# One fused transformer block pair: the expert stage gathers and adds only the slots in use, and adds whole 4 KB rows

## The chip, the cores and the metric

The kernel runs as one program on one core of a Trainium2 chip. The metric is the device time of one execution in microseconds (us). The engines named below are TensorE (PE in the rows, its weight loads PEld), VectorE (DVE), ScalarE (ACT), GpSimd (POOL) and SyncE (SP), and the core's 16 DMA engines, which every queue shares: q1 is the queue on which SP issues the weight loads, q0 the one on which GpSimd issues its indirect transfers.

## The reference, cut to what matters

A first block (a mixer of dilated attention and gated linear attention, then a mixture of experts) is followed by a second block (pooling and an RWKV recurrence). The change touches the mixture of experts alone:

```
T = 512 tokens, D = 1024, 32 experts, top 4 of each token
logits = xt @ router_w + router_b
top_v, top_i = top_k(logits, 4);  gates = softmax(top_v)
for each expert e, over the tokens that chose it:
    gu  = x[tokens] @ w_gate_up[e] + b_gate_up[e]          # 1024 x 2048
    act = min(gu[::2], 7) * sigmoid(1.702 * ..) * (clip(gu[1::2], -7, 7) + 1)
    out = act @ w_down[e] + b_down[e]                       # 1024 x 1024
    y[tokens] += gate * out
```

All is float32. An expert has 8 MB of gate-and-up weights and 4 MB of down weights, so 32 experts are 384 loads of 1 MB. On the reference's inputs the experts get 200, 146, 133, 125, 109, 86, 82, 82, 78, 76, 72, 65, 58, 57, 55, 54, 51, 48, 48, 48, 44, 42, 41, 40, 38, 37, 32, 26, 25, 16 and 13 tokens, and expert 31, which the kernel always takes first, 21.

## The kernel before, in words

The first part (to about 350 us) computes the mixer, its output projection and the router. Expert 31 is started before the routing is known (`FIXED`, three groups of 32 slots, computed by `counted` and `routing`); the other experts are sorted by their token counts, and rank r gets a fixed number of slots, `CAPS[r]`. `groups` cuts these into groups of m = 64 or m = 32 slots: 50 groups, 35 of 64 and 15 of 32, 2720 slots in all. A loop behind the planned part (`rest`) would compute tokens for which `CAPS` was too small.

A group passes these steps. `tokens` builds on VectorE a 0/1 matrix P (slot against token), TensorE multiplies it with a table to get for each slot the token's row and gate, VectorE turns them into an index tile `ix`, and GpSimd issues an indirect DMA (L1073) that gathers m rows of 4 KB of the normed activations into `xg`, which holds two groups, at partitions 0 and 64. Column 0 of `ix` is the row to gather, column 1 the row to add to; an empty slot points to one of 64 padding rows. `xT` transposes `xg` on TensorE (L1096) and ScalarE copies it out (L1098). `products` (L1120, L1123) multiplies by 1024 of the 2048 gate-and-up columns; the group has m stationary columns, and the 128/m column tiles of TensorE work on 128/m shares of the weight columns side by side, so the result lies as 128 partitions x 512 (m = 64) or 128 x 256 (m = 32). `gating` forms the activation, `actT` transposes it, `down` (L1166, L1172) does the last product in the same layout, ScalarE evicts it with the gate as scale into `o` (L1174), and GpSimd issues an indirect DMA that adds it into the accumulator in HBM (L1177): 128 descriptors, of 2 KB for m = 64, of 1 KB for m = 32.

TensorE's order is written by hand: `SEQ` lists 96 phases, (rank, phase) with phase 0 and 1 for the two halves of gate-and-up and 2 for down, interleaved over ranks. The weights of a phase are four loads of 1 MB on SP (L1037), in the same order, into a ring of 16 tiles; a load is issued only when the load four before it has landed (`FLIGHT`) and when its tile is free. `prep` runs `tokens` ahead of a rank's first phase by 40 units of a cost table, 8 for a group of 64 and 5 for one of 32. The other engines are ordered by a scheduler. The adds form a chain: each waits until the one before has landed. After the last add the accumulator is read back (L1455, `ym<-accd`) and the second block runs.

Of the kernel before, what the change touches and what calls it, by code (L numbers as in the profile page):

```python
# [10 lines left out]
F32 = mybir.dt.float32  # L11
# [4 lines left out]
AF = mybir.ActivationFunctionType  # L16
OP = mybir.AluOpType
# [64 lines left out]
def pre(tc, A, g):  # L82
# [294 lines left out]
    t4 = lambda name: prB.tile([128, 1024], F32, name=name, tag="t4", bufs=2)  # L377
    G = K()

    def gates():  # L380
# [46 lines left out]
    def dense():  # L427
# [39 lines left out]

        G.gates = 0

# [124 lines left out]
    prt_.__exit__(None, None, None)  # L594


CAPS = [96] + [224, 160, 160, 128, 128, 128] + [96] * 6 + [64] * 16 + [32] * 3
FIXED = 31
SEQ = [divmod(i, 3) for i in (
# [4 lines left out]
assert len(CAPS) == 32 and sorted(SEQ) == [(r, p) for r in range(32) for p in range(3)]  # L604


def groups(cap, first=False):
    if first:
        return [(s, 32) for s in range(0, cap, 32)]
    out, s = [], 0  # L610
    while s < cap:
        m = 64 if cap - s >= 64 else 32
        out.append((s, m))
        s += m
    return out

# [4 lines left out]
def route_consts():  # L621
# [395 lines left out]
class Moe:  # L1017
    def __init__(self, tc, A, g, work, ps, wtile):
        self.tc, self.A, self.g, self.w, self.ps, self.wtile = tc, A, g, work, ps, wtile
        self.nc = tc.nc  # L1020
        self.lead = 40
        self.ngu = 0
        self.half = 0
        self.loads, self.flow = [], True


# [20 lines left out]
        return [x for j in range(4) for x in self.load1(e, ph, j)]  # L1047


    def tokens(self, pos, aux, s0, m, gates=True):  # L1050
        nc, g, w, ps, c2 = self.nc, self.g, self.w, self.ps, self.g.c2
        dup = 128 // m
        T = pos.shape[1]
        P = w.tile([128, T, dup, m], BF, name="P", tag="P")
        nc.vector.tensor_tensor(P, c2("iota1")[:, None, None, s0:s0 + m].to_broadcast([128, T, dup, m]),
                                pos[:, :, :, None].to_broadcast([128, T, dup, m]), op=OP.is_equal)
        inf = ps.tile([128, 6], F32, name="inf", tag="tr", bufs=2)
        n = 6 if gates else 3
        for t in range(T):
            nc.tensor.matmul(inf[:, 0:n], P[:, t].rearrange("p d m -> p (d m)"), aux[:, t, 0:n], start=(t == 0), stop=(t == T - 1))  # L1060
        f = w.tile([128, 2], F32, name="inff", tag="inff", bufs=4)
        ix = w.tile([128, 2], I32, name="ix", tag="ix", bufs=14)

        nc.vector.tensor_reduce(out=f[:, 0:1], in_=inf[:, 0:2], axis=AX.X, op=OP.add)  # L1064
        nc.vector.tensor_copy(ix[:, 0:1], f[:, 0:1])  # L1065
        nc.vector.scalar_tensor_tensor(f[:, 1:2], inf[:, 2:3], c2(f"npad{m}"), c2(f"pad{m}"), op0=OP.mult, op1=OP.add)

        h = self.half
        if h == 0:
            self.xg = w.tile([128, 1024], F32, name="xg", tag="xg", bufs=3)  # L1070
        xg = self.xg[h:h + m]
        self.half = 64 - h
        nc.gpsimd.indirect_dma_start(out=xg, out_offset=None, in_=g.h2d[0:64 + 128 * T], in_offset=bass.IndirectOffsetOnAxis(ap=ix[0:m, 0:1], axis=0))  # L1073
        nc.vector.tensor_add(f[:, 0:1], f[:, 0:1], f[:, 1:2])
        nc.vector.scalar_tensor_tensor(ix[:, 1:2], f[:, 0:1], float(dup), c2(f"dg{m}"), op0=OP.mult, op1=OP.add)
        G = dict(m=m, xg=xg, h=h, ix=ix, P=P)
        if gates:
            self.gates(G, None, inf)
        return G
# [10 lines left out]

    def xT(self, G):
        nc, g, w, ps = self.nc, self.g, self.w, self.ps
        m, h = G['m'], G['h']
        pt = ps.tile([128, 8, m], F32, name="ptx", tag="tr", bufs=2)
        for k in range(8):
            nc.tensor.transpose(pt[:, k, :], G['xg'][:, k * 128:(k + 1) * 128], g.ident[h:h + m, h:h + m])  # L1096
        xT = w.tile([128, 8, m], F32, name="xT", tag="xT", bufs=7)
        nc.scalar.copy(xT, pt)  # L1098
        G['xT'] = xT

    def products(self, G, W, hf, sel):
        nc, g, ps = self.nc, self.g, self.ps
        m = G['m']
        cg = 128 // m
        n = 1024 // cg
        self.ngu += 1
        p = G['p', hf] = ps.tile([128, 512], F32, name="pgu", tag="mm" if self.ngu % 4 else "po", bufs=3 if self.ngu % 4 else 1)

        def part(w, c):

            if m == 64:
                return w[:, c * n:(c + 1) * n]
            return w.rearrange("p (a i k two) -> p a k i two", a=2, k=2, two=2)[:, c // 2, c % 2]

        def to(c):
            o = p[c * m:(c + 1) * m, :n]
            return o if m == 64 else o.rearrange("p (i two) -> p i two", two=2)

        for c in range(cg):
            nc.tensor.matmul(to(c), sel.to_broadcast([96, m]), part(g.bp[:, hf * 1024:(hf + 1) * 1024], c), start=True, stop=False)  # L1120
        for k in range(8):
            for c in range(cg):
                nc.tensor.matmul(to(c), G['xT'][:, k, :], part(W[k], c), start=False, stop=(k == 7))  # L1123
            yield

    def gating(self, G, hf):
# [32 lines left out]
    def down(self, G, W, sel, hold=False):  # L1159
        nc, g, w, ps = self.nc, self.g, self.w, self.ps  # L1160
        m = G['m']
        dg = 128 // m
        n = 1024 // dg
        p = ps.tile([128, 512], F32, name="pdn", tag="s", bufs=2)
        for c in range(dg):
            nc.tensor.matmul(p[c * m:(c + 1) * m, :n], sel.to_broadcast([96, m]), g.bp[:, 2048 + c * n:2048 + (c + 1) * n], start=True, stop=False)  # L1166
        for k in range(8):
            hf, q = k // 4, k % 4
            aT = G['aT', hf]
            lhs = aT[:, q % 2, (q // 2) * 64:(q // 2) * 64 + 64] if m == 64 else aT[:, 0, q * 32:(q + 1) * 32]  # L1170
            for c in range(dg):
                nc.tensor.matmul(p[c * m:(c + 1) * m, :n], lhs, W[k][:, c * n:(c + 1) * n], start=False, stop=(k == 7))  # L1172
        o = w.tile([128, 512], F32, name="o", tag="o", bufs=2)
        nc.scalar.activation(o[:, :n], p[:, :n], AF.Copy, scale=G['gate'][:, 0:1])  # L1174

        def add():
            return nc.gpsimd.indirect_dma_start(out=g.acc.rearrange("r (d n) -> (r d) n", n=n),  # L1177
                                                out_offset=bass.IndirectOffsetOnAxis(ap=G['ix'][:, 1:2], axis=0),
                                                in_=o[:, :n], in_offset=None, compute_op=OP.add)
        if hold:  # L1180
            self.held = add
        else:
            self.added = add()

    def run(self, moves):
        g, nc, ps = self.g, self.nc, self.ps
# [7 lines left out]

        T, W = {0: g.ahead}, {(0, 0): g.first[0], (0, 1): g.first[1], (0, 2): g.first[2]}

        cost = [sum((8 if m == 64 else 5) for _, m in groups(CAPS[r], r == 0)) for r, _ in SEQ]
        when = np.concatenate([[0], np.cumsum(cost)])
        first = {r: i for i, (r, ph) in enumerate(SEQ) if ph == 0}

        def prep(i):
            for x in sorted(first, key=first.get):
                if x not in T and when[first[x]] - when[i] <= self.lead:
                    T[x] = [self.tokens(g.ppr[:, :, x:x + 1], g.aux[:, :, x, :], s0, m) for s0, m in groups(CAPS[x])]

        def transposes(j):
            if j < len(SEQ) and SEQ[j][1] == 0:
# [1147 lines left out]
```

## Time and profile before

| | |
|---|---|
| median of 3 runs | 1835.36 us (1834.03 to 1836.15) |
| profiled execution, its own time | 1837.41 us |
| its span, first to last instruction | 1835.6 us |
| granted TensorE clock, mean | 0.952 |
| PE, DVE, ACT, POOL busy | 91%, 35%, 23%, 14% |
| HBM read, written | 494.05 MB, 26.36 MB |

The span has three parts. To about 400 us the mixer and the routing run; from 400 to 1440 us the experts; after that the second block. The profile gives for any stretch the busy time of each engine, the share of the 16 DMA engines and what they moved, the packets of each queue, and who waited for whom. A packet of a queue is what one DMA engine moves at a time; the share of a queue is the sum of its packets' times over the time of 16 engines.

### The profile page before, as it was taken

Reading aid. Unit: us, or ns where it says so; the run is one execution under the profiler, and the core shown is the slowest. Engines: PE = TensorE matmul, PEld = TensorE weight load, DVE = VectorE, ACT = ScalarE, POOL = GpSimd, SP = SyncE. Lnnn points to the kernel's source line nnn. Section 1 sums busy time; section 2 is a strip of 40 time slices with the busy share of each in tenths; the row PEclk is TensorE's granted clock in tenths of the full one; section 3 lists DMA queues with packets and bytes.
Section 4 is the critical chain, followed back from the end, with each engine's and each line's share of the span. In section 5 each row is a group of like instructions: output and inputs, shape, how many; then the busy total and the mean of one; then the engine's idle time right before and its main releaser. Section 6 shows DMA issues by size and latency. Waiting matters only on the chain. (4 is left out here: it accounts for less than half of the span.)

```text
span 1835.6 us, 28333 instructions
## 1 busy us (share of the span) xinstructions
PE 1669.5 (91%) x11329; PEld 892.5 (49%) x11329; DVE 648.7 (35%) x1639; ACT 420.4 (23%) x866; POOL 261.2 (14%) x189
## 2 busy tenths in 40 slices
PE   6889898989999999899998999999997489969988
PEld 4666576744333333233333333334332267757766
DVE  4636746642212111121211211212111367954353
ACT  4445554311111010011111011101011254322231
POOL 1734621011111001100110101020110100000000
PEclk9989889999999999999999999999999689979989
DMA  9654326799999999999999999999999934320151
GB/s 330 183 162 140 117 104 228 263 323 394 392 391 392 389 392 389 381 389 395 383 387 391 346 414 393 393 376 388 391 369 392 328 101 107 111 70 7 47 165 71
DMA packets 183961, 522.28 MB, mean 285 GB/s; under 512 B 28730, under 2 KB 71636, under 8 KB 167316
## 3 DMA queue, kind: packets, MB, share of 16 engines
q1 hardware_dynamic: 162562, 491.31, 71.0%
q0 software_dynamic: 10720, 22.29, 5.6%
q10 hardware_dynamic: 10546, 6.85, 1.3%
q8 instruction: 90, 1.47, 0.3%
q14 instruction: 43, 0.35, 0.1%
HBM read 494.05 MB, written 26.36 MB: 284 GB/s over the span
## 5 line engine op out<-in xcount | busy, mean ns | idle before, releaser
L1123 PE MATMUL pgu<-wra,xT 128*64 128x512 f32 (+1 forms) x1784 | 295.7, 522 | 11.1 <-DMA wra<-in_w_gate_up_dram 9.4
L1123 PE MATMUL pgu<-wrb,xT 128*32 128x256 f32 (+1 forms) x1936 | 281.9, 499 | 10.4 <-DMA wrb<-in_w_gate_up_dram 9.1
L1134 DVE TENSOR_SCALAR gm<-pgu 128x256 f32<-128x256 f32 (+1 forms) x100 | 38.4, 384 | 672.7 <-PE pgu L1123 672.7
L1123 PEld LDWEIGHTS pgu<-wra,xT 128*64 128x64 f32 (+1 forms) x1784 | 99.2, 127 | 172.6 <-issue 136.4
L1123 PEld LDWEIGHTS pgu<-wrb,xT 128*32 128x32 f32 (+1 forms) x1936 | 98.8, 125 | 162.5 <-issue 120.3
L1172 PE MATMUL pdn<-wra,aT 128*64 128x512 f32 (+1 forms) x1144 | 164.2, 488 | 1.6 <-DMA wra<-in_w_down_dram 1.5
L1177 POOL DMA_INDIRECT accd<-o,ix x50 | 78.7, 1574 | 606.9 <-ACT aT L1156 410.0
L1135 ACT ACTIVATE sg<-gm 128x256 f32<-128x256 f32 (+1 forms) x100 | 38.7, 387 | 357.3 <-DVE gm L1134 353.5
L1172 PE MATMUL pdn<-wrb,aT 128*64 128x512 f32 (+1 forms) x688 | 108.8, 505 | 6.8 <-DMA wrb<-in_w_down_dram 6.7
L1073 POOL DMA_INDIRECT xg<-h2d,ix x50 | 48.5, 970 | 406.7 <-DVE ix L1065 115.4
L1172 PEld LDWEIGHTS pdn<-wra,aT 128*64 128x64 f32 (+1 forms) x1144 | 58.3, 123 | 89.7 <-issue 71.8
L1174 ACT ACTIVATE o<-pdn,gate 128x512 f32<-128x512 f32 (+1 forms) x50 | 31.2, 624 | 276.4 <-PE pdn L1172 247.9
L1156 ACT COPY aT<-pta 128x256 f32<-128x256 f32 (+1 forms) x100 | 31.2, 341 | 268.0 <-PE pta L1154 267.5
L1507 PE MATMUL pf<-hh,wfh 128*128 128x512 f32 (+1 forms) x208 | 86.7, 417 | 0.5 <-ACT hh L1494 0.5
L1508 PE MATMUL pf<-hh,wfl 128*128 128x512 f32 (+1 forms) x208 | 83.0, 399 | 2.2 <-DVE wfl L1351 2.2
L1509 PE MATMUL pf<-hl,wfh 128*128 128x512 f32 (+1 forms) x208 | 82.6, 397 | 0.5 <-DVE hl L1495 0.5
L1123 PE MATMUL pgu<-wrx,xT 128*64 128x512 f32 (+1 forms) x440 | 69.3, 505 | 3.7 <-ACT xT L1098 2.1
L1064 DVE TENSOR_REDUCE inff<-inf 128x1 f32<-128x2 f32 x50 | 7.6, 152 | 174.4 <-PE inf L1060 167.8
L1172 PEld LDWEIGHTS pdn<-wrb,aT 128*64 128x64 f32 (+1 forms) x688 | 35.9, 126 | 68.2 <-issue 51.3
L1154 PEld LDWEIGHTS pta<-ct,act 128*128 128x128 f32 x170 | 24.2, 196 | 56.1 <-issue 52.6
L1507 PEld LDWEIGHTS pf<-hh,wfh 128*128 128x128 f32 x208 | 40.8, 196 | 12.1 <-issue 2.0
L1508 PEld LDWEIGHTS pf<-hh,wfl 128*128 128x128 f32 x208 | 40.8, 196 | 11.5 <-DVE wfl L1351 2.5
(514 smaller groups left out, 2531.5 us busy)
## 6 DMA issues: line engine op xcount, KB each, us to landing
wra<-in_w_gate_up_dram SPq DMA_DIRECT2D x125, 1024.0 KB
wrb<-in_w_gate_up_dram SPq DMA_DIRECT2D x104, 1024.0 KB
wra<-in_w_down_dram SPq DMA_DIRECT2D x63, 1024.0 KB
wrb<-in_w_down_dram SPq DMA_DIRECT2D x48, 1024.0 KB
wrx<-in_w_gate_up_dram SPq DMA_DIRECT2D x27, 1024.0 KB
wst<-in_w_in_dram SPq DMA_DIRECT2D x49, 512.0 KB
wrx<-in_w_down_dram SPq DMA_DIRECT2D x17, 1024.0 KB
wmb<-in_w_mod_dram SPq DMA_DIRECT2D x32, 512.0 KB
```

The costliest lines, as they stand in the source:

```text
L1073: nc.gpsimd.indirect_dma_start(out=xg, out_offset=None, in_=g.h2d[0:64 + 128 * T], in_offset=bass.IndirectOffsetOnAxis(ap=ix[0:m, 0:1], ax ...
L1123: nc.tensor.matmul(to(c), G['xT'][:, k, :], part(W[k], c), start=False, stop=(k == 7))
L1134: nc.vector.tensor_scalar(gm[:, :h], pv[:, :, 0], 7.0, None, op0=OP.min)
L1135: nc.scalar.activation(sg[:, :h], gm[:, :h], AF.Sigmoid, scale=1.702)
L1154: nc.tensor.transpose(pt[:, f, :], G['act', hf][:, f:128 * fh:fh], g.ident)
L1156: nc.scalar.copy(aT[:, 0:fh], pt[:, 0:fh])
L1172: nc.tensor.matmul(p[c * m:(c + 1) * m, :n], lhs, W[k][:, c * n:(c + 1) * n], start=False, stop=(k == 7))
L1174: nc.scalar.activation(o[:, :n], p[:, :n], AF.Copy, scale=G['gate'][:, 0:1])
L1177: return nc.gpsimd.indirect_dma_start(out=g.acc.rearrange("r (d n) -> (r d) n", n=n), out_offset=bass.IndirectOffsetOnAxis(ap=G['ix'][:, 1 ...
L1507: nc.tensor.matmul(p[:, a], hi[:, k, :], hh[:, k, a], start=(k == 0), stop=False)
L1508: nc.tensor.matmul(p[:, a], lo[:, k, :], hh[:, k, a], start=False, stop=False)
L1509: nc.tensor.matmul(p[:, a], hi[:, k, :], hl[:, k, a], start=False, stop=(k == 7))
```

## The change

`CAPS` gets a finer table, in multiples of 8; `groups` yields (start, m, used). The 50 groups stay 50, but now 32 of m = 64 and 18 of m = 32: the second group of rank 6 and the groups of ranks 27 and 28 go from 64 to 32. The slots in use are 2224: by group size 64 (19 groups), 56 (3), 48 (7), 40 (3), 32 (6), 24 (4), 16 (4) and 8 (4). Only the used slots are gathered, transposed and multiplied by gate-and-up; the unused part of P is set to zero. The column tiles keep their size and place. The down product is unchanged, but ScalarE evicts it in 128/m pieces that put the shares of a row side by side, so that a slot's result is one row of 1024 in one partition; `o` becomes one tile with two halves, partitions 0 to 63 and 64 to 127, used in turn. The add carries one descriptor of 4 KB for each used slot.

```diff
-CAPS = [96] + [224, 160, 160, 128, 128, 128] + [96] * 6 + [64] * 16 + [32] * 3
+CAPS = ([96] + [200, 152, 136, 128, 112, 88, 88, 88, 80, 80, 72, 72] + [64] * 2 + [56] * 3 + [48] * 6 + [40] * 3 + [32] * 3 + [16] * 2)
...
-        m = 64 if cap - s >= 64 else 32
-        out.append((s, m))
+        m = 64 if cap - s > 32 else 32
+        out.append((s, m, min(m, cap - s)))
...
-        nc.vector.tensor_tensor(P, c2("iota1")[:, None, None, s0:s0 + m].to_broadcast([128, T, dup, m]),
-                                pos[:, :, :, None].to_broadcast([128, T, dup, m]), op=OP.is_equal)
+        nc.vector.tensor_tensor(P[:, :, :, 0:used], c2("iota1")[:, None, None, s0:s0 + used].to_broadcast([128, T, dup, used]),
+                                pos[:, :, :, None].to_broadcast([128, T, dup, used]), op=OP.is_equal)
+        if used < m:
+            nc.vector.memset(P[:, :, :, used:m], 0.0)
...
-        xg = self.xg[h:h + m]
+        xg = self.xg[h:h + used]
         self.half = 64 - h
-        nc.gpsimd.indirect_dma_start(out=xg, out_offset=None, in_=g.h2d[0:64 + 128 * T], in_offset=bass.IndirectOffsetOnAxis(ap=ix[0:m, 0:1], axis=0))
-        nc.vector.tensor_add(f[:, 0:1], f[:, 0:1], f[:, 1:2])
-        nc.vector.scalar_tensor_tensor(ix[:, 1:2], f[:, 0:1], float(dup), c2(f"dg{m}"), op0=OP.mult, op1=OP.add)
+        nc.gpsimd.indirect_dma_start(out=xg, out_offset=None, in_=g.h2d[0:64 + 128 * T], in_offset=bass.IndirectOffsetOnAxis(ap=ix[0:used, 0:1], axis=0))
+        nc.vector.tensor_add(ix[:, 1:2], f[:, 0:1], f[:, 1:2])
...
-                nc.tensor.matmul(to(c), G['xT'][:, k, :], part(W[k], c), start=False, stop=(k == 7))
+                nc.tensor.matmul(to(c, used), G['xT'][:, k, :], part(W[k], c), start=False, stop=(k == 7))
...
-        o = w.tile([128, 512], F32, name="o", tag="o", bufs=2)
-        nc.scalar.activation(o[:, :n], p[:, :n], AF.Copy, scale=G['gate'][:, 0:1])
+        if self.o is None:
+            self.o = w.tile([128, 1024], F32, name="o", bufs=1)
+        o = self.o[self.oh:self.oh + 64]
+        self.oh = 64 - self.oh
+        for c in range(dg):
+            b = slice(c * m, (c + 1) * m)
+            nc.scalar.activation(o[0:m, c * n:(c + 1) * n], p[b, :n], AF.Copy, scale=G['gate'][b, 0:1])
+        u = G['used']
 
         def add():
-            return nc.gpsimd.indirect_dma_start(out=g.acc.rearrange("r (d n) -> (r d) n", n=n),
-                                                out_offset=bass.IndirectOffsetOnAxis(ap=G['ix'][:, 1:2], axis=0),
-                                                in_=o[:, :n], in_offset=None, compute_op=OP.add)
+            return nc.gpsimd.indirect_dma_start(out=g.acc, out_offset=bass.IndirectOffsetOnAxis(ap=G['ix'][0:u, 1:2], axis=0),
+                                                in_=o[0:u], in_offset=None, compute_op=OP.add)
...
-                    T[x] = [self.tokens(g.ppr[:, :, x:x + 1], g.aux[:, :, x, :], s0, m) for s0, m in groups(CAPS[x])]
+                    T[x] = [self.tokens(g.ppr[:, :, x:x + 1], g.aux[:, :, x, :], s0, m, u) for s0, m, u in groups(CAPS[x])]
```

The 384 weight loads stand on SP in the same order, into the same ring tiles, before and now. What moves is on GpSimd and ScalarE. GpSimd's indirect transfers near the end of the expert stage, before (`xg<-h2d,ix` is a gather, its size in rows x columns; `accd<-o,ix` an add, the size that of the accumulator as the index sees it, 1152 rows of 512 or 2304 of 256):

```order
L1073 DMA xg<-h2d,ix 64x1024
L1073 DMA xg<-h2d,ix 32x1024
L1177 DMA accd<-o,ix 2304x256
L1177 DMA accd<-o,ix 1152x512
L1073 DMA xg<-h2d,ix 64x1024
L1177 DMA accd<-o,ix 1152x512
```

and now, in the same place:

```order
L1078 DMA xg<-h2d,ix 64x1024
L1078 DMA xg<-h2d,ix 24x1024
L1189 DMA accd<-o,ix 576x1024 x2
L1078 DMA xg<-h2d,ix 64x1024
L1078 DMA xg<-h2d,ix 16x1024
L1189 DMA accd<-o,ix 576x1024
```

The gathers carry 24 and 16 rows where 32 stood, every add has the form of whole rows, and here and there a gather has changed places with an add. ScalarE in the middle of the stage, before (`o<-pdn,gate` is the eviction of the down product, `aT` and `xT` are copies of transposes, `sg` the sigmoid):

```order
L1174 ACTIVATE o<-pdn,gate 128x512
L1156 COPY aT<-pta 128x256
L1174 ACTIVATE o<-pdn,gate 128x512
L1098 COPY xT<-ptx 128x512
L1174 ACTIVATE o<-pdn,gate 128x256
L1135 ACTIVATE sg<-gm 128x256
```

and now:

```order
L1185 ACTIVATE o<-pdn,gate 64x512 x2
L1161 COPY aT<-pta 128x256
L1185 ACTIVATE o<-pdn,gate 64x512 x2
L1102 COPY xT<-ptx 128x384
L1185 ACTIVATE o<-pdn,gate 32x256 x4
L1140 ACTIVATE sg<-gm 128x256
```

Each eviction has become two or four instructions in the same place of the queue, and the copies behind it stand behind all of them.

## Rows read from the trace of the kernel before

**Rows 1.** The page's slices: the DMA engines' busy tenths over the span.

```profile
PEclk9989889999999999999999999999999689979989
DMA  9654326799999999999999999999999934320151
```

**Rows 2.** Windows by stage: busy us (instructions) of PE, PEld, DVE, ACT, POOL; PEclk, DMA, GB/s.

```profile
400.00:1400.00 1000.00, 962.10 (x6608) 367.06 (x6602) 183.81 (x679) 110.53 (x274) 117.78 (x91) 0.99 1.03 387
1400.00:1440.00 40.00, 27.73 (x232) 9.46 (x228) 3.75 (x12) 3.08 (x9) 1.56 (x1) 0.83 1.02 416
```

**Rows 3.** Waits of SP's queue, 400 to 1400: us in total, times, longest.

```profile
SPq L1037 <- DMA wra<-in_w_gate_up_dram: 284.5, 115, 5.8
SPq L1037 <- DMA wrb<-in_w_gate_up_dram: 187.3, 85, 5.5
...
SPq L1037 <- PE pdn L1172: 14.8, 10, 4.2
SPq L1037 <- PE pgu L1123: 12.6, 23, 3.7
```

**Rows 4.** DMA queues, 400 to 1400: packets, MB, share of 16 engines.

```profile
q1 hardware_dynamic: 79687, 364.69, 92.4%
q0 software_dynamic: 10130, 20.99, 9.8%
q8 instruction: 53, 0.87, 0.3%
```

**Rows 5.** DMA queues in a stretch without indirect transfers, 1276 to 1308.

```profile
q1 hardware_dynamic: 2184, 13.37, 100.5%
```

**Rows 6.** DMA queues around one gather of 64 rows, 451 to 456.

```profile
q0 software_dynamic: 80, 0.26, 17.4%
```

**Rows 7.** DMA queues around one add of 128 pieces of 2 KB, 527 to 533.

```profile
q0 software_dynamic: 144, 0.26, 23.7%
```

**Rows 8.** DMA queues around one add of 128 pieces of 1 KB, 481.5 to 486.

```profile
q0 software_dynamic: 144, 0.13, 18.2%
```

**Rows 9.** The page's row of queue q0 over the whole span.

```profile
q0 software_dynamic: 10720, 22.29, 5.6%
```

**Rows 10.** Groups of TensorE instructions by shape, 400 to 1400: count, busy us, mean ns.

```profile
L1123 PE MATMUL pgu<-wra,xT 128*64 128x512 f32 x1080 | 250.2, 602 | 10.8 <-DMA wra<-in_w_gate_up_dram 9.4 <-ACT xT L1098 1.4
...
L1172 PE MATMUL pdn<-wra,aT 128*64 128x512 f32 x576 | 129.8, 593 | 1.6 <-DMA wra<-in_w_down_dram 1.5
...
L1123 PE MATMUL pgu<-wra,xT 128*32 128x256 f32 x624 | 39.3, 390 | 0.0
...
L1172 PE MATMUL pdn<-wra,aT 128*32 128x256 f32 x560 | 32.5, 379 | 0.0
```

**Rows 11.** Evictions on ScalarE by shape, 400 to 1450.

```profile
L1174 ACT ACTIVATE o<-pdn,gate 128x512 f32<-128x512 f32 x35 | 24.1, 687 | 230.1 <-PE pdn L1172 205.6 <-issue 20.2 <-DMA accd<-o,ix 4.4
...
L1174 ACT ACTIVATE o<-pdn,gate 128x256 f32<-128x256 f32 x15 | 7.1, 475 | 46.2 <-PE pdn L1172 42.4 <-DMA accd<-o,ix 3.9
```

**Rows 12.** The page's groups of GpSimd's indirect transfers.

```profile
L1177 POOL DMA_INDIRECT accd<-o,ix x50 | 78.7, 1574 | 606.9 <-ACT aT L1156 410.0
...
L1073 POOL DMA_INDIRECT xg<-h2d,ix x50 | 48.5, 970 | 406.7 <-DVE ix L1065 115.4
```

**Rows 13.** VectorE's groups by shape, 400 to 1400.

```profile
L1055 DVE TENSOR_TENSOR P<-c2t,ppr 128x512 bf16<-128x512 f32 x41 | 27.7, 681 | 0.0
...
L1075 DVE SCALAR_TENSOR_TENSOR ix<-inff,c2t 128x1 int32<-128x1 f32 x43 | 6.6, 163 | 0.8
```

**Rows 14.** Timeline of the stage's end: start us, us, instruction, idle before.

```profile
1442.51 1.07 PE L1172 MATMUL pdn<-wrb,aT 128*32 128x256 f32 x16 [1.33 <-DMA wrb<-in_w_down_dram]
1443.65 0.47 ACT L1174 ACTIVATE o<-pdn,gate 128x256 f32<-128x256 f32 x1 [7.08 <-PE pdn L1172]
1444.40 1.55 POOL L1177 DMA_INDIRECT accd<-o,ix  x1 [29.11 <-ACT o L1174]
...
1449.69 0.33 SPq L1455 DMA_DIRECT2D ym<-accd  x1
```

More of the change, by code (lines that the diff above doesn't have):

```diff
@@ L608, in groups @@
     if first:
-        return [(s, 32) for s in range(0, cap, 32)]
+        return [(s, 32, 32) for s in range(0, cap, 32)]
     out, s = [], 0
     while s < cap:
-        m = 64 if cap - s >= 64 else 32
-        out.append((s, m))
+        m = 64 if cap - s > 32 else 32
+        out.append((s, m, min(m, cap - s)))
         s += m
@@ L1023, in __init__ @@
         self.half = 0
+        self.o, self.oh = None, 0
         self.loads, self.flow = [], True
@@ L1047, in load, with tokens @@
         return [x for j in range(4) for x in self.load1(e, ph, j)]
-    def tokens(self, pos, aux, s0, m, gates=True):
+    def tokens(self, pos, aux, s0, m, used=None, gates=True):
         nc, g, w, ps, c2 = self.nc, self.g, self.w, self.ps, self.g.c2
+        used = used or m
         dup = 128 // m
@@ L1070, in tokens @@
             self.xg = w.tile([128, 1024], F32, name="xg", tag="xg", bufs=3)
-        xg = self.xg[h:h + m]
+        xg = self.xg[h:h + used]
         self.half = 64 - h
-        nc.gpsimd.indirect_dma_start(out=xg, out_offset=None, in_=g.h2d[0:64 + 128 * T], in_offset=bass.IndirectOffsetOnAxis(ap=ix[0:m, 0:1], axis=0))
-        nc.vector.tensor_add(f[:, 0:1], f[:, 0:1], f[:, 1:2])
-        nc.vector.scalar_tensor_tensor(ix[:, 1:2], f[:, 0:1], float(dup), c2(f"dg{m}"), op0=OP.mult, op1=OP.add)
-        G = dict(m=m, xg=xg, h=h, ix=ix, P=P)
+        nc.gpsimd.indirect_dma_start(out=xg, out_offset=None, in_=g.h2d[0:64 + 128 * T], in_offset=bass.IndirectOffsetOnAxis(ap=ix[0:used, 0:1], axis=0))
+        nc.vector.tensor_add(ix[:, 1:2], f[:, 0:1], f[:, 1:2])
+        G = dict(m=m, used=used, xg=xg, h=h, ix=ix, P=P)
         if gates:
@@ L1092, in xT @@
         nc, g, w, ps = self.nc, self.g, self.w, self.ps
-        m, h = G['m'], G['h']
+        m, h = G['used'], G['h']
         pt = ps.tile([128, 8, m], F32, name="ptx", tag="tr", bufs=2)
@@ L1102, in products @@
         nc, g, ps = self.nc, self.g, self.ps
-        m = G['m']
+        m, used = G['m'], G['used']
         cg = 128 // m
@@ L1113, in part, with to @@
             return w.rearrange("p (a i k two) -> p a k i two", a=2, k=2, two=2)[:, c // 2, c % 2]
-        def to(c):
-            o = p[c * m:(c + 1) * m, :n]
+        def to(c, rows=m):
+            o = p[c * m:c * m + rows, :n]
             return o if m == 64 else o.rearrange("p (i two) -> p i two", two=2)
@@ L1195, in run @@
         T, W = {0: g.ahead}, {(0, 0): g.first[0], (0, 1): g.first[1], (0, 2): g.first[2]}
-        cost = [sum((8 if m == 64 else 5) for _, m in groups(CAPS[r], r == 0)) for r, _ in SEQ]
+        cost = [sum((8 if m == 64 else 5) for _, m, _ in groups(CAPS[r], r == 0)) for r, _ in SEQ]
         when = np.concatenate([[0], np.cumsum(cost)])
```

## The prediction

> **What bounds the kernel now.** I read the page's slices first: the DMA engines are full from the eleventh of the 40 slices to the thirty-second, and nowhere else for long [rows 1]. The table of stretches says the same in numbers: from 400 to 1400 us the DMA share is 1.03 (packets of different queues overlap a little, so it can pass 1) while TensorE is busy for 962 us of the 1000 [rows 2]. Both are near their limit, so the next view is the waits of SP, which issues the weights: it waits for earlier loads to land in hundreds of waits, the two largest rows alone being 284.5 and 187.3 us, and for TensorE to free a ring tile for 14.8 and 12.6 us [rows 3]. At the end of the stage TensorE waits for the last weights [rows 14] and has 12 us idle of 40 [rows 2]. So the expert stage ends when the last weight load has landed; TensorE follows with 38 us of slack in 1000.
>
> The queues of that stretch then tell what the DMA engines do besides weights: q1 moves 364.69 MB, and q0, the gathers and adds, takes 9.8% of the engines' time, 98 us, for 20.99 MB [rows 4]. In a stretch without indirect transfers q1 moves 13.37 MB in 32 us, 418 GB/s [rows 5]. At that rate the 364.69 MB would need 873 us. Of the 127 us above that, 98 are q0's own packets, some 4 those of q8 and a smaller queue (q8 has 0.3% [rows 4]), and 25 are weight packets that go slower beside the others. That is the stock from which the change can take.
>
> **The change part by part.** *Bytes.* 50 gathers and 50 adds move 2720 rows of 4 KB each way, 22.28 MB, which is the 22.29 MB of the page's row [rows 9]; now 2224 rows each way, 18.22 MB, so 4.06 MB less. If cost follows bytes, 98 us for 20.99 MB are 4.67 us per MB and 19.0 us go; with the 25 us of slowed weight packets put down to q0 as well, 5.86 us per MB and 23.8 us.
>
> *Packets.* The same by pieces. One gather of 64 rows takes 17.4% of 16 engines in 5 us, 13.9 engine-us: 217 ns a packet of 4 KB [rows 6] (80 packets are counted: 64 rows and 16 that only signal). One add of 128 x 2 KB takes 22.8 engine-us, 178 ns a packet [rows 7]; one of 128 x 1 KB 13.1, 102 ns [rows 8]. Before, the gathers are 2720 x 217 ns / 16 = 36.9 us and the adds (35 x 128 x 178 + 15 x 128 x 102) / 16 = 62.1 us, 99.0 in all, against the 5.6% of 1835.6 us, 102.8, that the page has for q0 [rows 9]. An add packet of 4 KB is not in the trace. The line through 102 and 178 gives 178 + 2 x 76 = 330 ns. It is bounded below by the gather's 217 (a packet that adds should not be cheaper than one that copies) and above by four times the 1 KB packet, 408. With 330 the adds become 2224 x 330 / 16 = 45.9 us, 16.2 less; the gathers 2224 x 217 / 16 = 30.2, 6.7 less; together 22.9 us. With 217 it is 31.9 + 6.7 = 38.6; with 408 and gathers that do not get cheaper at all with fewer rows, 5.4. I take 22, between the 19.0 and 23.8 of the bytes and next to the 22.9 of the packets; 5 and 39 are kept for the range.
>
> No transfer in the trace has a row count other than 32, 64 or 128, so no row shows how 8, 24, 40 or 56 rows spread over the engines. The Trainium skill (DMA: Bandwidth & Descriptors, "Why a DMA increments its semaphore by 16 and not by 1") says that a transfer runs on the largest number of engines up to 16 that divides its row count, which would put 40 rows on 10 engines, 56 on 14, 24 on 12 and 8 on 8. By that rule the busiest engine would have as much as before in some groups; the rival below gives its time.
>
> *TensorE.* A group's half of gate-and-up is 32 instructions at 250.2 us / 1080, 7.41 us, for m = 64, and 64 at 39.3 / 624, 4.03 us, for m = 32; down is 7.21 and 3.71 [rows 10]. Three groups narrower are 3 x (2 x 3.38 + 3.50) = 30.8 us less work. Fewer stationary columns in a tile of the same size change nothing in the 512 or 256 columns that stream, so I count nothing for them. I also count nothing for the 30.8 us: TensorE is not what ends the stage. But they matter as cover: with about 22 us fewer to hide in, TensorE's slack goes from 38 to about 47 us.
>
> *ScalarE.* The evictions were 35 x 0.687 + 15 x 0.475 = 31.2 us [rows 11]. The new shapes are not in the trace; if a piece costs what the same free size costs over 128 partitions, they are 64 x 0.687 + 72 x 0.475 = 78.2 us, 47 more; if time goes with the elements, none. I take 47. ScalarE is busy 110.5 us in 1000 [rows 2], so it fits; the copies of transposes that stand behind an eviction come up to 0.7 or 1.4 us later, and TensorE waits for those. All 47 on TensorE's path would use up the 47 us of slack, no more. At the very end it is seen: the last eviction (0.47 us) becomes four, 1.4 us later, while the last transfer's issue on GpSimd falls from 1.55 us towards the gather's 0.97 [rows 12, 14]. Net +0.8 us, taken as 1.
>
> *VectorE and GpSimd.* One index operation of 163 ns goes from each group; 25 groups get a memset, at most the 681 ns of the whole matrix [rows 13]; VectorE is busy 184 of 1000 us. GpSimd's issue of an add falls from 1574 ns towards 970 [rows 12]. Both are idle most of the time; nothing is counted. The adds still form one chain, each waiting for the landing of the one before, 50 over a thousand us, and the two halves of `o` wait as the two buffers did.
>
> *Sum.* -22 + 1 = -21 us. Against the profiled execution's 1837.4 that is 1816.4; its time lay 2.0 above the median of the runs, so I predict 1814.4.
>
> **Rivals.** *Uneven engines.* A weight load is complete when all its parts are, so what counts of a small transfer may be its busiest engine. Then 40 and 56 rows cost as 64, 24 as 32, 8 as 16: 2384 rows. Adds 2384 x 330 / 16 = 49.2, gathers 32.3: 17.5 us less, 1818.9. For it: the loads in flight are only four. Against it: different transfers can load different engines, and four loads in flight even that out. This is where the engine rule of the Trainium skill would show.
>
> *A price per transfer.* If the 98 us belong to 100 transfers and not to their rows, nothing is won: 1835. Against it: the 1 KB add, with as many packets as the 2 KB add and half the bytes, takes 13.1 engine-us to 22.8 [rows 7, 8].
>
> *Dear adds, slower than before.* A 4 KB add packet, read from 64 partitions where 128 served, might stretch far above the line. Against the 6.7 us that the gathers give, adds of 2224 x t / 16 break even with 62.1 + 6.7 at t = 495 ns; above that the kernel is slower. At 660 ns, twice the line, adds are 91.7 us: +29.6 - 6.7 + 1 = +24, 1859. For it: no row has such a packet, and the line through two points may bend. Against it: 102 to 178 ns for double the bytes is less than double.
>
> *Overflow: the change does not do what it says.* Eight ranks have exactly as many tokens as slots (200, 72, 48 three times, 40, 32, 16). One token more on one of them runs the loop behind the planned part: 12 loads of 1.05 MB at 418 GB/s, 30 us, and nothing beside them: 1845 or more. For it: the table is exact. Against it: the counts follow from the inputs.
>
> *Cheaper adds.* 217 ns a packet: 1837.4 - 38.6 + 1 - 2.0, about 1798.
>
> **How the numbers follow.** The forecast has 0.62, its own range 1808 to 1822; uneven engines 0.18; a price per transfer 0.09; dear adds 0.04; overflow 0.02; cheaper adds 0.05. Faster by over 0.2% (3.7 us, about what a measurement of this kernel can tell from no change) are the forecast, uneven engines, cheaper adds and 0.02 of the price per transfer, 0.87; the same are the rest of that case, 0.07; slower 0.06. The range for 8 in 10 goes from 1801 to 1829: the cheap adds and the price per transfer lie outside, half-way cases towards both inside.
>
> **What the profile after would show.** q0 with 2224 + 2224 + 1600 = 6048 packets and 18.2 MB over the span, at about 4.3% of the engines (79 us) where 5.6% stood; around one add of 64 rows, packets near 330 ns; the end of the expert stage (`ym<-accd`) near 1429 us where 1449.7 stood, and everything behind it unchanged; SP's waits for TensorE no longer; TensorE's idle time in the stage up, not down; exactly 50 gathers and 50 adds. I am wrong if the stage's end does not move with q0's share: if q0's packets take 23 us less and the stage ends less than 14 us earlier, TensorE or ScalarE was in the way. I am wrong in the size if a 4 KB add packet is far from 330 ns, or if small gathers take the engines as long as gathers of 32 or 64 rows.

## The result and the profile after

The changed kernel takes 1813.11 us (median of 4 runs, 1809.89 to 1820.19) against 1835.76 (4 runs of before, 1834.03 to 1837.81): a ratio of 0.9879, 95% interval 0.9854 to 0.9904. I had said 1814.4, 1801 to 1829. The total came out; several of the terms it was summed from did not.

The profiled execution took 1809.89 us, its span 1808.1. Against the profiled execution of before the span is 27.5 us shorter, in two pieces: the expert stage ends 15.8 us earlier (`ym<-accd` at 1433.88, 1449.69 before [rows 14]), and the second block, which the change does not touch, takes 374.2 us instead of 385.9.

What was predicted of the transfers is there. First the page's row of q0 of the kernel after, over its whole span (packets, MB, share of 16 engines), to be read against [rows 9]:

```profile
q0 software_dynamic: 6368, 18.23, 4.4%
```

4.4% of 1808.1 us is 79.6 us of 16 engines, 23.2 less than before; I had said 79. The packets are 320 more than the 6048 I counted, all of them small; with the 2384 rows of the rival *Uneven engines* in place of the 2224 moved, 2 x 2384 + 1600 = 6368 comes out exactly. Now one add of 64 whole rows, 740 to 744 us:

```profile
q0 software_dynamic: 80, 0.26, 33.0%
```

33.0% of 4 us on 16 engines are 21.1 engine-us for 64 packets of 4 KB, 330 ns each, the value taken from the line through [rows 7, 8].

The windows by stage and the queues from 400 to 1400, after, against [rows 2, 4]:

```profile
400.00:1400.00 1000.00, 951.66 (x6985) 358.93 (x6979) 172.47 (x664) 155.04 (x362) 108.41 (x91) 0.98 1.02 390
1400.00:1440.00 40.00, 19.86 (x222) 7.88 (x218) 5.41 (x14) 9.31 (x18) 6.28 (x3) 0.71 0.90 348
```

```profile
q1 hardware_dynamic: 81059, 371.72, 93.9%
q0 software_dynamic: 6059, 17.45, 7.7%
```

The weights go 7.03 MB further in the same 1000 us. At the quiet rate of 418 GB/s [rows 5] that is 16.8 us, about the stage's gain again, and 4 us less than q0's packets gave up in this window (9.8% to 7.7%, 21 us). ScalarE is 44.5 us busier. The next two views show where time was still lost: SP's waits for TensorE (400 to 1400), and TensorE's waits for ScalarE's copies (400 to 1440); each row has the total, the times and the longest.

```profile
SPq L1039 <- PE pdn L1177: 15.0, 14, 6.7
SPq L1039 <- PE pgu L1128: 14.5, 23, 3.4
```

```profile
PE ptx L1100 <- ACT aT L1161: 9.9, 9, 1.9
...
PE pta L1159 <- ACT aT L1161: 5.1, 7, 1.7
```

I had said that SP would no longer wait for TensorE. It waits as long as before [rows 3]. The transposes wait up to 1.9 us for a copy on ScalarE; the same two rows of before are these:

```profile
PE ptx L1096 <- ACT aT L1156: 2.2, 6, 0.5
...
PE pta L1154 <- ACT aT L1156: 1.7, 6, 0.4
```

The evictions by shape, after, against [rows 11], and the end of the stage, against [rows 14]:

```profile
L1185 ACT ACTIVATE o<-pdn,gate 64x512 f32<-64x512 f32 x64 | 43.7, 683 | 193.0 <-PE pdn L1177 173.1 <-issue 17.6 <-DMA accd<-o,ix 1.5
L1185 ACT ACTIVATE o<-pdn,gate 32x256 f32<-32x256 f32 x72 | 33.5, 466 | 47.0 <-PE pdn L1177 41.1 <-issue 5.0
```

```profile
1426.23 1.07 PE L1177 MATMUL pdn<-wrb,aT 128*32 128x256 f32 x16 [1.26 <-DMA wrb<-in_w_down_dram]
1427.37 1.90 ACT L1185 ACTIVATE o<-pdn,gate 32x256 f32<-32x256 f32 x4 [6.86 <-PE pdn L1177]
1429.55 1.33 POOL L1189 DMA_INDIRECT accd<-o,ix  x1 [24.90 <-ACT o L1185]
...
1433.88 1.28 SPq L1466 DMA_DIRECT2D ym<-accd  x3
```

A piece of 64 x 512 takes 683 ns, where 128 x 512 took 687: time goes with the elements of a partition, 77.2 us in all (78.2 expected). The four last pieces take 1.90 us where one took 0.47, and the issue behind them falls from 1.55 to 1.33.

### The profile page after: what moved, and what is told of

It reads as the page before. It is cut to its first block, busy times and chain, and to the rows that moved or that the text cites. A ratio compares the mean times of both kernels' runs of the same rounds, so it can differ in the third digit from the quotient of the medians.

```text
span 1808.1 us, 28999 instructions
## 1 busy us (share of the span) xinstructions
PE 1638.4 (91%) x11629; PEld 870.8 (48%) x11629; DVE 635.6 (35%) x1614; ACT 465.6 (26%) x952; POOL 252.0 (14%) x189
## 3 DMA queue, kind: packets, MB, share of 16 engines
q0 software_dynamic: 6368, 18.23, 4.4%
## 4 chain that ended last, share of the span: by engine, by line
PE 53%; DMA 22%; DVE 10%; issue 4%; ACT 4%; POOL 1%; ACTq 0%; SPq 0%; DVEq 0%; POOLq 0%
PE pgu L1128 22%; PE pdn L1177 11%; DMA wrb<-in_w_gate_up_dram 5%; DMA wra<-in_w_gate_up_dram 4%; DMA wra<-in_w_down_dram 3%; DMA wrx<-in_w_gate_up_dram 3%; DMA wrb<-in_w_down_dram 2%; PE pf L1518 1%; DVE prod L1806 1%; PE pf L1519 1%; PE pf L1520 1%; DMA wst<-in_w_out_dram 1%; PE ptx L1100 1%; PE pgu L1125 1%; ACT o L1185 1%
## 5 line engine op out<-in xcount | busy, mean ns | idle before, releaser
L1128 PE MATMUL pgu<-wra,xT 128*64 128x512 f32 (+7 forms) x1872 | 285.0, 504 | 7.9 <-DMA wra<-in_w_gate_up_dram 5.2
L1128 PE MATMUL pgu<-wrb,xT 128*64 128x512 f32 (+7 forms) x2016 | 274.0, 488 | 5.6 <-DMA wrb<-in_w_gate_up_dram 4.9
L1128 PEld LDWEIGHTS pgu<-wra,xT 128*64 128x64 f32 (+7 forms) x1872 | 92.9, 117 | 166.3 <-issue 124.0
L1128 PEld LDWEIGHTS pgu<-wrb,xT 128*64 128x64 f32 (+7 forms) x2016 | 92.8, 116 | 156.4 <-issue 115.9
L1177 PE MATMUL pdn<-wra,aT 128*32 128x256 f32 (+1 forms) x1200 | 162.9, 485 | 0.8 <-DMA wra<-in_w_down_dram 0.7
L1185 ACT ACTIVATE o<-pdn,gate 64x512 f32<-64x512 f32 (+1 forms) x136 | 77.2, 568 | 239.9 <-PE pdn L1177 214.2
L1177 PE MATMUL pdn<-wrb,aT 128*32 128x256 f32 (+1 forms) x712 | 108.1, 506 | 4.6 <-DMA wrb<-in_w_down_dram 4.5
L1177 PEld LDWEIGHTS pdn<-wra,aT 128*32 128x32 f32 (+1 forms) x1200 | 58.6, 124 | 87.0 <-issue 66.6
L1128 PE MATMUL pgu<-wrx,xT 128*64 128x512 f32 (+7 forms) x464 | 70.2, 503 | 1.9 <-DMA wrx<-in_w_gate_up_dram 1.4
L1159 PEld LDWEIGHTS pta<-ct,act 128*128 128x128 f32 x164 | 23.2, 193 | 58.4 <-issue 50.3
L1159 PE MATMUL pta<-ct,act 128*128 128x128 f32 x164 | 37.9, 322 | 10.7 <-DVE act L1144 5.5
```

The source lines that it names most:

```text
L1128: nc.tensor.matmul(to(c, used), G['xT'][:, k, :], part(W[k], c), start=False, stop=(k == 7))
L1159: nc.tensor.transpose(pt[:, f, :], G['act', hf][:, f:128 * fh:fh], g.ident)
L1185: nc.scalar.activation(o[0:m, c * n:(c + 1) * n], p[b, :n], AF.Copy, scale=G['gate'][b, 0:1])
```

## The experiments

"Stage end" is the start of `ym<-accd` and "behind" the time from there to the span's end, both of the one profiled execution; "SP waits" are SP's waits for `pdn` and `pgu`, 400 to 1400. "Order" says whose order the instructions of SP, ScalarE and VectorE have behind the stage, by the programs; TensorE's and GpSimd's order there is the same in before, after, e1 to e4, e7 and e8.

| kernel | median us (runs) | stage end | behind | SP waits | order |
|---|---|---|---|---|---|
| before | 1835.8 (4); 1835.6 to 1836.4 beside the experiments | 1449.7 | 385.9 | 27.4 | before |
| after | 1813.1 (4) | 1433.9 | 374.2 | 29.5 | changed |
| e1 narrow only | 1823.5 (6) | 1444.0 | 377.7 | 5.2 | changed |
| e2 rows of 4 KB only | 1836.1 (12) | 1458.2 | 377.3 | 60.9 | a third |
| e3 narrow, rows of 4 KB | 1825.5 (6) | 1445.4 | 378.7 | 34.2 | changed |
| e4 sixteens | 1820.6 (6) | 1440.1 | 380.6 | 42.6 | before |
| e5 after, split evictions | 1812.5 (5) | 1428.4 | 380.6 | 12.4 | changed |
| e6 e2, split evictions | 1828.0 (12) | 1451.5 | 378.9 | 20.5 | changed |
| e7 pair, 2296 rows | 1815.4 (6) | 1438.2 | 374.0 | 28.8 | changed |
| e8 pair, 2312 rows | 1820.4 (6) | 1430.9 | 385.0 | 16.9 | before |
| e9 e5 and 50 gathers of 32 | 1857.1 (4) | 1471.2 | 382.0 | 10.0 | before |
| e10 e5 and 50 gathers of 40 | 1881.1 (4) | 1503.5 | 377.9 | 16.7 | changed |
| e11 e5 and 50 gathers of 41 | 2066.9 (4) | 1696.8 | 372.9 | 105.0 | changed |
| e12 gathers only | 1824.2 (6) | 1437.2 | 383.6 | 10.0 | before |

A single stage end is good to a few us: e8 moves 16 rows more than e7 and ended 7.3 us earlier. So sizes are taken from medians where these can tell.

**The parts one by one (e1 to e4).** e1 is the kernel before with narrower groups:

```diff
-CAPS = [96] + [224, 160, 160, 128, 128, 128] + [96] * 6 + [64] * 16 + [32] * 3
+CAPS = [96, 224, 160, 160, 128, 128] + [96] * 7 + [64] * 14 + [32] * 5
```

> The kernel before with one edit: the three groups narrower, whole groups gathered and added, adds still in pieces of 1 and 2 KB. By rows and by busiest engine alike the expert stage gains 3 x 0.61 us of adds (22.8 engine-us against 13.1, over 16) and 96 x 217 ns / 16 = 1.3 us of gathers, 3 us: it ends near 1446.6 us instead of 1449.7. Behind the stage this kernel's instructions stand in the order of the changed kernel (the loads and splits of the last w_out parts come later on SP, ScalarE and VectorE), not in that of before. Theory order: the 11.7 us that the changed kernel gained behind the stage come from that order, so this one takes 374 us from ym<-accd to the end, in all near 1821. Rival chance or clock: the order is nothing, 386 us behind the stage, in all near 1833.

1823.5 us, ratio 0.9918 (0.9899 to 0.9937), 12.6 less than before. It is more than 3 and near what the theory of order gave, but the division was off: the stage ended 5.7 us earlier and the rest took 8.2 less. SP's waits for TensorE fell from 27.4 us to 5.2, in e1:

```profile
SPq L1037 <- PE pdn L1172: 2.9, 5, 1.9
SPq L1037 <- PE pgu L1123: 2.3, 8, 0.4
```

e2 is the changed kernel with the old `CAPS`, so that every slot of a group counts as used; e3 has e1's table in the changed kernel:

> One edit alone: results leave as whole rows of 4 KB; slots and groups as before (2720 rows each way). Adds fall from 62.1 engine-us to 2720 x 327 ns / 16 = 55.6 (327 ns is the median packet in the changed kernel's trace), the end of the stage costs 1 us more: it ends near 1444. If instead the pieces of a row make no difference, 1450. Behind the stage the order is a third one; between 374 and 386 us there. Total 1818 to 1831.

> Whole rows of 4 KB and three groups narrower, but whole groups of 32 and 64 gathered and added (2624 rows). Adds 2624 x 327 / 16 = 53.6 us, 8.5 less than before, gathers 1.3 less, 1 us more at the end: the stage ends near 1441. What is left to the changed kernel's 1433.9 is the part of the used slots: 7 us measured then, where by rows it is 400 x (327 + 217) / 16 = 13.6 us and by the busiest engine (2384 in place of 2224) 8.2. Behind the stage the order is that of the changed kernel: by the theory of order 374 us, in all near 1817; else 386, near 1829.

e2: 1836.1 us, ratio 0.9996 (0.9981 to 1.0011): nothing, and its stage ended 8.5 us later than before, not 6 earlier. q0 takes 5.2% of 1835.5 us, 95.4 us, so the packets did give back the 7 us. SP waits for TensorE twice as long as before, in e2:

```profile
SPq L1039 <- PE pgu L1128: 35.9, 29, 6.4
SPq L1039 <- PE pdn L1177: 25.0, 16, 7.1
```

e3: 1825.5 us, 0.9935 (0.9916 to 0.9954), 2.0 above e1 although its adds take 6.7 us less by packets. Both say that whole rows, with their evictions in pieces, cost as much as the packets win, or more: beside the 1 us counted for the end of the stage, 7.7 us in e3; in e2 about 6 by the medians, and 14 by the stage's end, part of which the shorter time behind it gives back.

e4 has slots in multiples of 16:

```diff
-CAPS = ([96] + [200, 152, 136, 128, 112, 88, 88, 88, 80, 80, 72, 72] + [64] * 2 + [56] * 3 + [48] * 6 + [40] * 3 + [32] * 3 + [16] * 2)
+CAPS = [96, 208, 160, 144, 128, 112, 96, 96, 96, 80, 80, 80, 80] + [64] * 5 + [48] * 9 + [32] * 3 + [16] * 2
```

> The changed kernel with slots in multiples of 16 in place of 8: 2336 rows each way, 112 more than in the changed kernel (40 becomes 48, 56 becomes 64, 24 becomes 32, 8 becomes 16). By rows: 112 x (327 + 217) / 16 = 3.8 us more, the stage ends near 1437.7. By the busiest engine: 40 rows stand on ten engines with four each, as 64 rows do, 48 on sixteen with three, so this kernel costs 2336 rows against 2384: 1.6 us less, the stage ends near 1432.3. Behind the stage its instructions stand exactly in the order of the kernel before. Theory order: 386 us there, in all near 1820, slower than the changed kernel although the stage is not. Rival chance or clock: 374 us, in all near 1808.

1820.6 us, ratio 0.9922 (0.9893 to 0.9951). The total is as the theory of order and the busiest engine gave it, but the parts are not: the stage ended at 1440.1, and 380.6 us came behind it. That decided nothing about rows, and e7 and e8 were made for the order.

**Late TensorE (e5, e6).** Every second piece of an eviction goes to VectorE, in the changed kernel and in e2:

```diff
         for c in range(dg):
             b = slice(c * m, (c + 1) * m)
-            nc.scalar.activation(o[0:m, c * n:(c + 1) * n], p[b, :n], AF.Copy, scale=G['gate'][b, 0:1])
+            if c % 2 == 0:
+                nc.scalar.activation(o[0:m, c * n:(c + 1) * n], p[b, :n], AF.Copy, scale=G['gate'][b, 0:1])
+            else:
+                nc.vector.tensor_scalar(o[0:m, c * n:(c + 1) * n], p[b, :n], G['gate'][b, 0:1], None, op0=OP.mult)
```

> The changed kernel, with every second piece of an eviction of pdn on VectorE, the others on ScalarE as they were. Theory late TensorE: the pieces that stand one behind another on ScalarE hold pdn and the copies of the transposes, TensorE frees weight tiles later, and SP waits for it: 29.5 us (pdn and pgu) in the changed kernel and 61 in the kernel with 4 KB rows alone, against 5.2 us in the one with narrower groups alone. Halved pieces bring these waits under 15 us and the stage ends 5 to 8 us earlier, near 1427; in all near 1806. Rival, transfers alone: only the rows that are moved count; these waits hide under the transfers, and it stays near 1434 and 1813.

> The kernel with 4 KB rows alone, with every second piece of an eviction on VectorE. Theory late TensorE: that kernel's stage ended at 1458 though q0's packets took 7 us less than before, because SP waited 61 us for pdn and pgu where before it waited 27. With the split the waits fall to 30 or below and the stage ends near 1447, its gain of 7 us by packets seen less something; behind it stands the order of the changed kernel (377 us), in all near 1826. Rival, dear 4 KB rows: an add of whole rows slows the weights beside it, whoever evicts: 1458 and 1836 again, less at most some us for the order.

e6: 1828.0 us (12 runs, 1823.0 to 1833.1) against e2's 1836.1 (12 runs, 1831.6 to 1840.9): 8.2 less, with the same rows and the same packets; behind the stage, where the order is another, its profile is no shorter (378.9 and 377.3). What waits in e6:

```profile
SPq L1039 <- PE pdn L1177: 11.6, 14, 3.6
SPq L1039 <- PE pgu L1128: 8.9, 10, 5.1
```

```profile
PE ptx L1100 <- ACT aT L1161: 2.5, 6, 0.6
...
PE pta L1159 <- ACT aT L1161: 2.0, 7, 0.4
```

In e2 these two rows of TensorE are 8.6 and 5.1. So in e2 it is the pieces on ScalarE, and not the 4 KB rows on the DMA engines. e5: 1812.5 us (1807.7 to 1812.9), ratio 0.9863 (0.9837 to 0.9888). The waits fell as expected (12.4 us) and its stage ended 5.5 us earlier, but the median is only 0.6 below the changed kernel's: behind the stage its profile has 380.6 us instead of 374.2. Half of the expectation fails there. Of these 6.4 us, 5.8 are TensorE's own busy time for the same 2208 instructions (327.8 us at a granted clock of 0.91, 322.0 at 0.93); why the clock differs is open, and the kernel after has only four runs, over 10 us.

**The order behind the stage (e7, e8).** Two tables of slots that differ in the 12th and 13th entry:

```diff
-CAPS = ([96] + [200, 152, 136, 128, 112, 96, 96, 96, 80, 80, 72, 72] + [64] * 5 + [48] * 9 + [32] * 3 + [16] * 2)
+CAPS = ([96] + [200, 152, 136, 128, 112, 96, 96, 96, 80, 80, 80, 80] + [64] * 5 + [48] * 9 + [32] * 3 + [16] * 2)
```

> Of a pair: slots of 2296 rows, groups as in the changed kernel (24 to 32, 56 to 64, 40 to 48; only the last 8 of 72 stay). Behind the stage its instructions stand in the order of the changed kernel. Stage: by rows 72 x (327 + 217) / 16 = 2.4 us later than the changed kernel, by the busiest engine 1.6 us earlier (no group of 40 left). Theory order: 374 to 379 us from ym<-accd to the end; in all 1813 to 1817.

> The other of the pair: 16 rows more (72 to 80 for two ranks, 0.5 us by rows, nothing by the busiest engine); TensorE's and GpSimd's orders are the same as in the first, and behind the stage the loads and splits of the last w_out parts stand as in the kernel before. Theory order: 381 to 386 us behind the stage and a total 6 us above its partner's. Rival chance: no difference beyond 1 us between the two medians.

1815.4 us (1814.0 to 1817.8) and 1820.4 (1817.7 to 1826.9): 5.0 us, in place of 6. In both programs the work is the same but for 16 rows, and in the stage the traces have the instructions of every engine in the same order; behind it the scheduler put loads of `wst` and the splits of it (`w2h`, `w2l`) elsewhere. The profiles have the difference behind the stage, 374.0 and 385.0 us. The windows show it, two of 25 us and the whole stretch behind the stage, first of e7, then of e8 (the last columns are the clock, the DMA share and GB/s):

```profile
1638.20:1663.20 25.00, 23.96 (x223) 19.29 (x221) 9.47 (x15) 6.01 (x10) 0.96 (x1) 0.97 0.03 11
...
1738.20:1763.20 25.00, 22.11 (x111) 14.75 (x112) 17.33 (x33) 10.06 (x20) 0.00 (x0) 0.93 0.51 154
...
1438.23:1812.20 373.97, 321.16 (x2208) 253.59 (x2208) 228.15 (x394) 127.80 (x212) 6.28 (x3) 0.93 0.33 98
```

```profile
1630.90:1655.90 25.00, 24.23 (x225) 19.36 (x223) 9.62 (x16) 4.13 (x7) 0.96 (x1) 0.86 0.03 12
...
1730.90:1755.90 25.00, 21.47 (x149) 17.80 (x149) 15.70 (x27) 11.27 (x20) 0.00 (x0) 0.74 0.69 210
...
1430.90:1815.90 385.00, 330.61 (x2208) 264.20 (x2208) 228.84 (x394) 127.80 (x212) 6.28 (x3) 0.89 0.32 95
```

At the same distance from the stage's end, 300 us, TensorE's granted clock is 0.93 in one and 0.74 in the other, a mean over times at 2.4 and at 1.2 GHz. In before that window has 0.69 and in after 0.93, but e4, with the order of before, has 0.91, so one window does not stand for the order. Over the whole stretch TensorE is busy 9.4 us longer in e8 for the same 2208 instructions, at 0.89 where e7 has 0.93; that is most of the 11.0 us between the two profiles. Waits are the smaller part: from 250 us behind the stage on TensorE waited 2.1 us for `MJ` and 2.0 for `tok` in e8, 0.8 and none in e7, but 1.5 and 0.5 for `w2h` and `w2l` in e7 and none in e8. So in this pair the time behind the stage goes with a lower clock; how the order brings that about was not tried. Over the five kernels with the order of before the time behind the stage is 380.6 to 385.9 us at clocks of 0.89 to 0.91, over the eight with the changed order 372.9 to 380.6 at 0.91 to 0.93.

**Rows or the busiest engine (e9 to e11).** To e5, ahead of each gather, a second one into the same place (32, 40 or 41 rows; the rest unchanged; the second waits until the first has landed):

```diff
+        nc.gpsimd.indirect_dma_start(out=self.xg[h:h + 40], out_offset=None, in_=g.h2d[0:64 + 128 * T], in_offset=bass.IndirectOffsetOnAxis(ap=ix[0:40, 0:1], axis=0))
         nc.gpsimd.indirect_dma_start(out=xg, out_offset=None, in_=g.h2d[0:64 + 128 * T], in_offset=bass.IndirectOffsetOnAxis(ap=ix[0:used, 0:1], axis=0))
```

> The changed kernel with split evictions, and ahead of each of the 50 gathers one more of 32 rows into the same place, which leaves the output as it is. 50 x 32 x 217 ns / 16 = 21.7 us of DMA time by rows, and as much by the busiest engine (two rows on each of sixteen): the stage ends near 1450 where 1428.4 stood. Behind the stage the order is that of before, so some 5 us more there than in the kernel with split evictions: in all near 1839. Rival, these gathers are hidden: 1428 and 1817.

> The same with 40 rows in place of 32; the order behind the stage is that of the changed kernel. By rows 50 x 40 x 217 ns / 16 = 27.1 us: the stage ends near 1455.5, 5.4 us behind the kernel with 32 rows, and the total is near 1840. By the busiest engine (ten engines with four rows each) 43.4 us: 1471.8, 21.7 us behind that kernel, total near 1856.

> The same with 41 rows, a prime number. By rows 27.8 us, the stage ends near 1456 and the total is near 1840, as with 40. If the number of engines must divide the rows, all 41 stand on one engine, 41 x 217 ns = 8.9 us for each gather; if that engine's time counted in full the stage would be hundreds of us longer, and any clear part of it (total above 1860) is for the busiest engine.

Stage ends of 1471.2, 1503.5 and 1696.8 us; e5's is 1428.4. The three are far apart, so it is not the rows alone. 32 rows cost 0.86 us for each gather, 40 cost 1.50 (1.75 times, where rows give 1.25 and the busiest engine 2), 41 cost 5.4. The first two are above what I expected: 32 rows twice the 0.43 us of their packets, and e10's stage ends 32 us behind e9's, where I had 5.4 by rows and 21.7 by the busiest engine. SP waits 10.0 and 16.7 us for TensorE in e9 and e10 and the DMA share stays at 1.02, so these two are mostly a matter of the transfers, though GpSimd also stands 105 and 140 us in all waiting for the extra gathers to land. In e11 it stands 621 us, and TensorE waits for gathers as well, 136.4 us for `xg` from 400 to 1400, so these 5.4 us are not the engines' time alone. One gather of 41 rows in e11, 725 to 742 us, and GpSimd's wait for it:

```profile
q0 software_dynamic: 672, 0.17, 5.1%
```

```profile
721.78 1.45 POOL L1078 DMA_INDIRECT xg<-h2d,ix  x1 [24.21 <-PE pgu L1129]
741.51 0.88 POOL L1079 DMA_INDIRECT xg<-h2d,ix  x1 [18.29 <-DMA xg<-h2d,ix]
```

5.1% of 17 us on 16 engines are 13.9 us of engine time, 8.0 for the 41 rows and 6.0 for 631 small packets. The trace's packets have the 41 rows one after another, never two at once, a start every 0.35 us from 726.8 to 740.5: the work of one engine, with other packets between. 672 packets are 16 x 42, and e10 has 80 = 16 x 5 for each extra gather of 40 rows where e9 has 48 = 16 x 3 for 32, as if each of sixteen engines had as many as the busiest, and one that signals. The Trainium skill (DMA: Bandwidth & Descriptors, "Why a DMA increments its semaphore by 16 and not by 1") has the rule that the number of engines divides the rows, one engine for 41, ten for 40, sixteen for 32. The order of the three stage ends agrees. It adds that transfers on fewer than sixteen take consecutive engines in turn, by which 40 rows would cost less than twice 32 when several are under way; no row here names an engine.

**Gathers alone (e12).** The changed kernel with the eviction and the add of before:

```diff
-        for c in range(dg):
-            b = slice(c * m, (c + 1) * m)
-            nc.scalar.activation(o[0:m, c * n:(c + 1) * n], p[b, :n], AF.Copy, scale=G['gate'][b, 0:1])
+        o = w.tile([128, 512], F32, name="o", tag="o", bufs=2)
+        nc.scalar.activation(o[:, :n], p[:, :n], AF.Copy, scale=G['gate'][:, 0:1])
```

> The changed kernel's narrower groups and gathers of the used slots alone, with the adds of the kernel before: whole groups, in pieces of 1 and 2 KB, one eviction each. The order behind the stage is that of before. Against the kernel before: 8 us for the narrower groups (the 12.6 measured, less some 5 that came from the order) and 400 x 217 ns / 16 = 5.4 us for gathers: near 1823. Against the two kernels with rows of 4 KB, used slots and the same order behind the stage (1820.6 and 1820.4) that leaves 2 to 3 us for the whole change of the adds, where packets alone say 16: theory late TensorE, the pieces of the evictions take the rest. Rival, the adds gain by their packets: this kernel is 10 us or more behind them, 1830 or above.

1824.2 us, ratio 0.9931 (0.9909 to 0.9954), as expected. Behind the stage it has the order of before, and so has e8 at 1820.4: what was done to the adds is worth 3.8 us there (good to some 3 us), where by packets e8's 2312 rows have 13.0 us less of adds (60.3 in pieces, 47.3) and 1.2 more of gathers.

No kernel is clearly better than the changed one; e5 is level with it.

## Why the prediction was right in sum, and where not in its steps

The path from before to after in medians, each step between kernels of one order or with the pair's 5.0 us taken off:

| step | I counted | measured | from |
|---|---|---|---|
| order behind the stage | 0 | -5.0 | e7 against e8 |
| three groups narrower | -3.1 | -7.6 | e1 against before, less the 5.0 |
| adds as whole rows of 4 KB, end of the stage | -5.7 | +2.0 | e3 against e1 |
| used slots only | -13.6 | -12.4 | after against e3 |
| sum | -22.4 | -23.0 | measured -22.65 |

The first column divides the sum's terms with 327 ns for an add packet, the median of all of them. So 1814.4 is a right total of four terms, of which the last alone holds; that the total came out is luck in part. By the scatter of the runs (95%) the steps are good to 3, 4, 4 and 7 us, the last because the kernel after has four runs.

- *Bytes and packets, -22 us.* The size of q0's time was right (-23.2), and so was 330 ns. The step to the stage's end failed: my mark was 14 us of gain for 23, and 15.8 passes it by little. What was late next is the term below.
- *ScalarE, +47 us counted as nothing.* The 47 came (46.0 more), and I had seen that TensorE would wait for the copies, but priced it at nothing, since TensorE had slack. It has slack on average; at those places SP waited for its tiles. Cost: 7.7 us (e3 against e1, beside the 5.7 expected), 8.2 (e6 against e2). In the changed kernel the same split shortened the stage by 5.5 us, but of that e5's median shows 0.6.
- *TensorE, 30.8 us counted as nothing.* The narrower groups gave 7.6 us (5.7 by the stage's end), 4.5 more than their transfers, and took 22 us from SP's waits. So SP's 27.4 us of waits for TensorE [rows 3] look like a price, and I read them as cover; the 4.5 us are barely clear of the scatter.
- *"Everything behind it unchanged"* failed: -5.0 us by the pair, -11.7 in the two profiles.
- *The tail, +1 us.* From the start of the last group of products to `ym<-accd` 7.18 us passed before [rows 14] and 7.65 after: 0.5, right. So was TensorE's idle time, up from 38 to 48 us of the 1000.
- *Uneven engines.* The engines do share like that (e9 to e11, and the 6368 packets of q0), but what it costs the change can't be told from the forecast. The used slots gave 12.4 us, where rows give 13.6 and the busiest engine 8.2, and the 7 us of scatter cover both. e7, which has no group of 40 and 72 rows more, is 2.2 us slower than the changed kernel, where rows have 2.4 more and the busiest engine 1.6 less; that is inside the scatter as well.
- *The other rivals* fell: adds cost 330 ns and not 217 or 495, and there are exactly 50 gathers and 50 adds. A price that goes by transfers alone is out too, as 50 gathers more cost 42.8, 75.1 or 268.4 us by their rows (e9 to e11); a part for each transfer beside the rows is not excluded, since 32 rows cost twice their packets.

## What to carry to other kernels

When two resources are both near full, price every edit on both: a wait of 15 us on the engine that "has slack" is where the next gain goes, and work added to a side engine costs where its results are waited for, not where its busy share says. Read an equal sum only after each term has been run alone; here two errors of about 8 and 10 us hid each other. Compare also the order of what an edit does not touch: a scheduler moved it, and 5 us with it.

## What the runs showed of the hardware

- Small gathers in a full stage can cost twice their packets' own time: in e9 the 50 gathers of 32 rows added 20.5 us of q0's time (5.4% of 1853.2 us against 4.4% of 1809.0) and 42.8 us to the stage's end. What the other half is was not tried.
- Row counts decide how an indirect transfer spreads: 41 rows came one behind another and cost 5.4 us in the stage where 40 cost 1.5.
- An eviction's time goes with the elements of one partition: 64 x 512 683 ns, 128 x 512 687; 32 x 256 466, 128 x 256 475.
- TensorE's granted clock from 400 to 1400 us is 0.98 in all six kernels whose pieces are on ScalarE alone (after, e2, e3, e4, e7, e8) and 0.99 in before, e1, e5, e6, e9 and e12. In the six TensorE's `ptx` transposes wait 8.6 to 9.9 us for copies `aT` (400 to 1440), in the others 2.0 to 2.5: longer pauses and a little more time at 1.2 GHz go together. 0.01 of 1000 us is the size of the 8 us; what is cause there was not tried.
- TensorE's time for the same 2208 instructions behind the stage runs from 320.3 us at a granted clock of 0.93 (e11) to 330.6 at 0.89 (e8).
